# Sample-token matmuls of 32 and 64 columns, issued in alternation between column groups

## The chip, the cores and the metric

The kernel runs on one core of one Trainium2 chip. The metric is the device time of the whole program in microseconds (us); lower is better. Times of a stretch come from one profiled execution of the same program. PE is the matrix engine (TensorE), DVE, ACT and POOL are the vector, scalar and GpSimd engines, SP issues most transfers.

## The reference, cut to what matters

One inference step of a one-layer decoder for 1024 prompt tokens and for 8 sequences of 4 new tokens each (32 "sample" tokens). A layer adds three things to the stream: a token mixer (a gated delta rule with 4 heads beside local attention with windows 128, 512 and 2048 at strides 1, 4 and 16), cross-attention to 256 memory rows, and a mixture of tiny experts (PEER). For the sample tokens every sequence has its own state, its own window cache and its own memory rows:

```python
# gated delta rule, one token after another
S_t = a_t S_{t-1} + k_t u_t^T
u_t = beta_t (v_t - a_t S_{t-1}^T k_t)
o_t = S_t^T q_t
# local attention of the new tokens over the cache and themselves
s = einsum('bthc,btmhc->bhtm', q, kg) * dh**-0.5
p = exp(s - logsumexp(s));  o = einsum('bhtm,btmhc->bthc', p, vg)
# cross-attention
p = softmax(einsum('bthc,bmhc->bhtm', q, k_mem) * dh**-0.5)
o = einsum('bhtm,bmhc->bthc', p, v_mem)
```

So a product for the sample tokens has 8 parts (sequences, or positions of a window), each with its own key or value matrix. The kernel puts the queries of one part into a 32- or 64-column stationary tile that is zero elsewhere, and adds up 8 or 32 matmuls in one PSUM tile.

## The kernel before, in words

The prompt is worked in three groups of tokens (384, 384, 256); the sample tokens ride with the second group. `base` runs for each group: input norm and projections, then three rounds of delta-rule chunks (`delta_block`) and one window of local attention each (`windows(i)`), the output projection, cross-attention and the routing of the experts. After the third group a dense phase (`dense`) goes through all experts for part of the tokens. The experts of the other tokens are read row by row: `experts` and `experts_v` gather one row per token from HBM on POOL (L1248, tile `gat`, four buffers), and DVE multiplies it (L1257) or adds it up (L1406). These gathers run beside everything else, from about 700 us on. `mm` counts matmul work and notes a DVE instruction as an anchor each time enough of it has gone by; `paced` issues one gather step after each anchor.

The program is written in one order and then put in order engine by engine by a scheduler that follows a model of the times. Each engine's queue is fixed after that: an instruction that waits holds up what stands behind it on its engine. Tiles come from pools with fixed numbers of buffers that are taken in turn, and a load waits until the last reader of the buffer's old tile is done.

Four places touch the sample tokens' small matmuls. All operands are fp32; the trace shows two records for each such matmul.

- `delta_sample` (L629 to L677), once, about 1142 to 1192 us. For each of four heads: load the states `s` (512 KB, tile `zz`), 8 matmuls of 32 columns of the keys with the states into `r[:, 0]` (L657), DVE makes `x` (L660), one matmul gives `r[:, 1]` (L661), ACT copies it to `us` (L662), 8 matmuls of the queries with the states into `r[:, 2]` (L664), one more (L665), ACT copies it out (L666). Then eight 128-column matmuls make the new states (L672), which go back to HBM (L676). All of `r` that is used lies on partitions 0 to 31.
- `s_scores` (L921 to L949), once for each window. The four heads are two pairs; pair 0 fills partitions 0 to 63 of one PSUM tile (`tp`), pair 1 partitions 64 to 127. For windows 1 and 2 each pair has four steps `t8`: load 512 KB of keys into a `zz` tile (L938), make the stationary tile `z` (POOL memset L905, DVE copies L909), 8 matmuls of 64 columns (L941). Window 0 has one step for each pair. Pair 0 goes through all its steps, then pair 1.
- `win_sample` (L951 to L992), the same with values (L971, L975).
- `mem_sample` (L1095 to L1135): four heads, head `hd` on partitions `32*hd` to `32*hd+31`; for each of 8 sequences two halves of keys or values of 512 KB are loaded (L1144) into seven buffers (`O`, `wk`, `wv`), and 8 matmuls of 32 columns follow, the loop over heads outside and over the two halves of the sum inside.

`zz` has three buffers (`ZB = 3`), shared by the states, keys and values here. `halves_load` and `ztile` hand out the tiles.

## Time and profile before

| what | before |
|---|---|
| three runs | 4059.99, 4069.17, 4082.94 us |
| median | 4069.17 us |
| span of the profiled execution, first to last instruction | 4081.0 us |
| share of the span: PE, DVE, ACT, POOL | 89%, 72%, 36%, 36% |
| moved by DMA | 1101.38 MB, mean 270 GB/s |
| matmul records of PE | 18530 |

The profiled execution's own time is not given apart from its span; the slowest of the three runs is 1.9 us above that span, and the median 11.8 us below it. A busy share is an average over stages with different limits, so the stages are read one by one: the table of engines by stretch tells which engine is full, the groups by shape tell what a kind of matmul costs, the timelines tell what a matmul waited for, and the chain of waits tells whose work ended a stretch. In the lists, "x16" is 16 records, that is 8 fp32 matmuls, and a bracket at a row's end is idle time of the engine before that row with what ended it.

### The profile page before, as it was taken

To read this page: it belongs to the slowest core of one execution; us is meant where nothing else is said; L and a number is where in the kernel's file an instruction comes from. 1 tells how busy PE (TensorE), PEld (TensorE's weight loads), DVE (VectorE), ACT (ScalarE), POOL (GpSimd) and SP (SyncE) were. 2 spreads that over 40 slices of the span, in tenths; PEclk is the share of its full clock that TensorE was granted. 3 is DMA by queue.
4 is the path that set the end of the run, shared out by engine and by line. 5 is a ranking of instruction groups with operands and counts; after the bars stand their busy time and mean duration, and the time that the engine had idled before them with its cause. 6 is when DMAs were issued, how large, how long until landed. Compare 5 with 4: busy or idle time off the path is not lost.

```text
span 4081.0 us, 54174 instructions
## 1 busy us (share of the span) xinstructions
PE 3619.0 (89%) x18530; PEld 2976.6 (73%) x18530; DVE 2938.5 (72%) x6731; ACT 1470.6 (36%) x3278; POOL 1477.9 (36%) x1317
## 2 busy tenths in 40 slices
PE   8999988888999878774799887899969999999999
PEld 8988878666777634443677776788858888888887
DVE  4422338876575655789977887899768888887886
ACT  4434344333223011211245687223443333333333
POOL 0000000253334545454334443444544444444442
PEclk9998899789878988787788898999989999999998
DMA  6532554376668988886577888999999999999995
GB/s 219 188 117 92 189 196 146 123 254 206 230 229 298 334 331 310 296 297 201 189 237 267 290 321 330 327 349 330 348 323 336 342 342 340 340 339 321 338 332 198
DMA packets 383525, 1101.38 MB, mean 270 GB/s; under 512 B 40528, under 2 KB 147728, under 8 KB 379536
## 3 DMA queue, kind: packets, MB, share of 16 engines
q0 software_dynamic: 168736, 614.54, 42.5%
q1 hardware_dynamic: 214512, 483.37, 33.9%
q8 instruction: 147, 2.41, 0.2%
q14 instruction: 130, 1.06, 0.1%
HBM read 1025.37 MB, written 117.02 MB: 280 GB/s over the span
## 4 chain that ended last, share of the span: by engine, by line
PE 49%; DMA 18%; DVE 14%; issue 10%; POOL 4%; ACT 4%; POOLq 0%; SPq 0%; DVEq 0%; ACTq 0%
PE ps L148 29%; PE dl L148 11%; DMA gat<-expert_u,eid 5%; DMA gat<-expert_v,eid 5%; PE tp L148 4%; POOL gat L1248 4%; PE po L148 3%; DVE gat L1257 2%; DVE acc L1406 2%; DMA gat<-expert_v,e 1%; DMA O<-cmv 1%; PE tp L846 1%; DVE tk L1155 1%; DMA gscr<-C 1%; DVE tmp L419 1%
## 5 line engine op out<-in xcount | busy, mean ns | idle before, releaser
L1248 POOL DMA_INDIRECT gat<-expert_u,eid x512 | 625.1, 1221 | 819.1 <-DVE hid L1257 569.0
L1248 POOL DMA_INDIRECT gat<-expert_v,eid x512 | 627.7, 1226 | 771.8 <-DVE acc L1406 420.3
L1257 DVE CUSTOM_DVE_ANT_0 gat<-gat,fr 128x1024 f32<-128x1024 f32 x576 | 697.1, 1219 | 220.5 <-DMA gat<-expert_u,eid 209.2
L1406 DVE SCALAR_TENSOR_TENSOR acc<-gat,hid,acc 128x1024 f32<-128x1024 f32 x576 | 737.2, 1280 | 146.1 <-DMA gat<-expert_v,eid 128.9
L148 PE MATMUL dl<-dtm,dtm 128*128 128x128 f32 (+3 forms) x2336 | 328.2, 292 | 36.6 <-ACT C L1313 18.1
L148 PE MATMUL ps<-C,w 128*128 128x416 f32 x768 | 309.8, 562 | 43.2 <-DMA w<-w_pq 31.6
L148 PEld LDWEIGHTS dl<-dtm,dtm 128*128 128x128 f32 (+2 forms) x2336 | 307.7, 206 | 54.9 <-ACT C L1313 20.5
L148 PE MATMUL dl<-O,dtm 128*128 128x480 f32 x1152 | 286.3, 379 | 0.0
L148 PEld LDWEIGHTS ps<-C,w 128*128 128x128 f32 x768 | 156.7, 209 | 175.0 <-issue 127.3
L1266 ACT ACTIVATE dtm<-w 128x512 fp32r<-128x512 f32 x288 | 178.0, 629 | 269.7 <-PE dl L148 183.6
L148 PE MATMUL ps<-C,wk 128*128 128x480 f32 x1024 | 249.3, 385 | 21.2 <-ACT C L1266 12.7
L148 PE MATMUL ps<-C,zz 128*128 128x480 f32 (+1 forms) x1088 | 263.1, 379 | 1.4 <-DVE zz L1267 1.4
L1266 ACT ACTIVATE wk<-wv 128x1024 fp32r<-128x1024 f32 x128 | 135.8, 1061 | 332.9 <-PE ps L148 219.8
L148 PE MATMUL ps<-B,wk 128*128 128x480 f32 x1024 | 244.9, 381 | 0.2 <-DVE B L1267 0.2
L148 PEld LDWEIGHTS dl<-O,dtm 128*128 128x128 f32 x1152 | 216.6, 188 | 33.5
L148 PE MATMUL tp<-O,dtm 128*128 128x480 f32 x768 | 208.3, 386 | 32.1 <-ACT O L1266 30.1
L148 PEld LDWEIGHTS ps<-C,wk 128*128 128x128 f32 x1024 | 191.2, 190 | 56.4 <-ACT C L1266 13.6
L148 PEld LDWEIGHTS ps<-C,zz 128*128 128x128 f32 x1088 | 204.1, 188 | 32.3 <-DVE zz L1267 1.8
L1267 DVE TENSOR_TENSOR dtm<-w,dtm 128x512 fp32r<-128x512 f32 x288 | 197.0, 688 | 41.4 <-PE dl L148 16.8
L148 PE MATMUL ps<-A,w 128*128 128x256 f32 (+1 forms) x768 | 197.4, 415 | 21.2 <-ACT tmp L406 13.7
L148 PEld LDWEIGHTS ps<-B,wk 128*128 128x128 f32 x1024 | 193.8, 189 | 30.2 <-DVE B L1267 0.9
L148 PE MATMUL ps<-O,dtm 128*128 128x480 f32 x768 | 210.5, 379 | 0.2 <-DVE vzs L1394 0.2
(479 smaller groups left out, 6665.4 us busy)
## 6 DMA issues: line engine op xcount, KB each, us to landing
wv<-expert_uT SPq DMA_DIRECT2D x128, 512.0 KB
w<-expert_v SPq DMA_DIRECT2D x128, 512.0 KB
w<-w_in SPq DMA_DIRECT2D x102, 512.0 KB
s_win<-cache_win SPq DMA_DIRECT2D x64, 512.0 KB
A<-gscr SPq DMA_DIRECT2D x32, 960.0 KB
gscr<-C SPq DMA_DIRECT2D x13, 2048.0 KB
w<-w_pq SPq DMA_DIRECT2D x48, 512.0 KB
uscr<-tmp SPq DMA_DIRECT2D x60, 240.0 KB
```

What stands on the lines that cost most here:

```text
L148: x = self.nc.tensor.matmul(out, lhsT, rhs, **kw)
L419: nc.vector.scalar_tensor_tensor(av, xv(j), cw[:, ch, j:j + 1], av, op0=ALU.mult, op1=ALU.add)
L846: nc.tensor.transpose(tp[:r, c, :], e[:lq, j, o:o + r], C["ident"][:lq, :lq])
L1155: nc.vector.match_replace(out=w, in_to_replace=vals[:, 0:8], in_values=src, imm_value=-3.0e38)
L1248: return self.nc.gpsimd.indirect_dma_start(out=dst, out_offset=None, in_=src, in_offset=bass.IndirectOffsetOnAxis(ap=idx, axis=0))
L1257: nc.vector.tensor_tensor_reduce(out=u, in0=u, in1=fr, scale=1.0, scalar=0.0, op0=ALU.mult, op1=ALU.add, accum_out=hid[:, s:s + 1])
L1266: nc.scalar.activation(hi, x, AF.Copy)
L1267: nc.vector.tensor_tensor(lo, x, hi.bitcast(F32), op=ALU.subtract)
L1406: nc.vector.scalar_tensor_tensor(acc, v, c[:, s:s + 1], acc, op0=ALU.mult, op1=ALU.add)
```

## The change: what it does

It changes orders and one place in PSUM; no matmul, load or copy is added or taken away.

1. `delta_sample`: the queries' 8 matmuls now write partitions 32 to 63 of `r` and are issued alternately with the keys' 8, ahead of the DVE step.
2. `s_scores` and `win_sample`: the loop over the two pairs is inside the loop over the steps. Each step loads two tiles, makes two stationary tiles, and alternates the matmuls of the pairs.
3. `mem_sample`: the loop over the heads is inside the loop over the two halves of the sum.

```diff
@@ delta_sample
             for b in range(NB):
-                self.mm(r[:m, 0], kq[:, 0, b], s[:, b], start=b == 0, stop=b == NB - 1)
+                self.mm(r[:m, 0], kq[:, 0, b], s[:, b], start=b == 0, stop=b == NB - 1, skip_group_check=True)
+                self.mm(r[m:2 * m, 2], kq[:, 1, b], s[:, b], start=b == 0, stop=False, skip_group_check=True)
...
             nc.scalar.activation(us[:m], r[:m, 1], AF.Copy)
-            for b in range(NB):
-                self.mm(r[:m, 2], kq[:, 1, b], s[:, b], start=b == 0, stop=False)
-            self.mm(r[:m, 2], aT[:m, h], us[:m], start=False, stop=True)
-            nc.scalar.activation(on[:m, h], r[:m, 2], AF.Copy)
+            self.mm(r[m:2 * m, 2], aT[:m, h], us[:m], start=False, stop=True, skip_group_check=True)
+            nc.scalar.activation(on[:m, h], r[m:2 * m, 2], AF.Copy)
@@ s_scores
+        q = [wq[pr][:, L:] for pr in range(2)]
+        srcs = [[(hsl[hh], hh, x[hsl[hh]]) for hh in range(2)] for x in q]
+        for t8 in range(1 if g == 0 else 4):
+            kk, z = [], []
+            for pr in range(2):
+                kk.append(self.ztile())
+                nc.sync.dma_start(kk[pr], I["ck0"][pr] if g == 0 else I[f"ck{g}"][pr, t8])
+                z.append(self.diag_b(srcs[pr]) if g == 0 else self.diag(pr, t8, srcs[pr]))
+            for t in range(8):
+                for pr in range(2):
+                    self.mm(s[pr * DH:(pr + 1) * DH, :P], z[pr][:, t], kk[pr][:, t], start=t8 == 0 and t == 0, stop=False, skip_group_check=True)
         for pr in range(2):
-            rows = slice(pr * DH, (pr + 1) * DH)
-            q = wq[pr][:, L:]
-            srcs = [(hsl[hh], hh, q[hsl[hh]]) for hh in range(2)]
-            if g == 0:
...
-            else:
-                for t8 in range(4):
-                    kk = self.ztile()
-                    nc.sync.dma_start(kk, I[f"ck{g}"][pr, t8])
-                    z = self.diag(pr, t8, srcs)
-                    for t in range(8):
-                        self.mm(s[rows, :P], z[:, t], kk[:, t], start=t8 == 0 and t == 0, stop=False, skip_group_check=True)
...
@@ win_sample
+        for t8 in range(n8):
+            vv, z = [], []
+            for pr in range(2):
+                vv.append(self.ztile())
+                nc.sync.dma_start(vv[pr], I["cv0"][pr] if g == 0 else I[f"cv{g}"][pr, t8])
+                z.append(self.diag_b(srcs[pr]) if g == 0 else self.diag(pr, t8, srcs[pr]))
+            for t in range(8):
+                for pr in range(2):
+                    self.mm(op[rows[pr]], z[pr][:, t], vv[pr][:, t], start=False, stop=t8 == n8 - 1 and t == 7, skip_group_check=True)
@@ mem_sample, keys; the values likewise with m for c
-            for hd in range(4):
-                for c in range(2):
+            for c in range(2):
+                for hd in range(4):
                     self.mm(s[hd * NS:(hd + 1) * NS], qz[hd][:, c, b], ks[hd // 2][:, 2 * (hd % 2) + c, :],
                                      start=b == 0 and c == 0, stop=b == NB - 1 and c == 1, skip_group_check=True)
```

How it moves instructions, in three places. First PE in `delta_sample`, head 1 (tile `dl_8061` is its `r`, `zz_8056` its states, `dtm_8058` its masked keys and queries). Before:

```order
L148 MATMUL dl_8048<-dtm_8023,dtm_8046 128x128 x4
L148 MATMUL dl_8061<-zz_8056,dtm_8058 32x128 x8
L148 MATMUL dl_8061<-dtm_8070,dtm_7982 32x128
L148 MATMUL dl_8061<-zz_8056,dtm_8058 32x128 x8
L148 MATMUL dl_8061<-dtm_8070,dtm_7922 32x128
L148 MATMUL dl_8086<-dtm_8070,dtm_8084 128x128 x4
L148 MATMUL dl_8095<-dtm_8070,dtm_8093 128x128 x4
```

With the change:

```order
L148 MATMUL dl_8061<-zz_8056,dtm_8058 32x128 x16
L148 MATMUL ps_8630<-cf,ml_8604 64x128 x6
L148 MATMUL ps_8638<-cf,ml_8604 64x128 x6
L148 MATMUL dl_8061<-dtm_8078,dtm_7982 32x128
L148 MATMUL dl_8061<-dtm_8078,dtm_7922 32x128
L148 MATMUL dl_8086<-dtm_8078,dtm_8084 128x128 x4
L148 MATMUL dl_8095<-dtm_8078,dtm_8093 128x128 x4
```

The second group of eight has moved ahead of the one matmul that needs DVE's `x`, and nothing stands any more between that one and the one that needs ACT's `us`.

Second, PE in `s_scores` of window 2 (`tp_9623` is the scores' tile, each `zz` one loaded tile of keys, `ks` the new tokens' keys). Before:

```order
L148 MATMUL tp_9623<-zz_9624,tmp_9626 64x128 x8
L148 MATMUL tp_9623<-zz_9638,tmp_9640 64x128 x8
L148 MATMUL tp_9623<-zz_9652,tmp_9654 64x128 x6
L148 MATMUL ps_9589<-cf,ml_9579 64x128 x6
L148 MATMUL ps_9597<-cf,ml_9579 64x128 x6
L148 MATMUL tp_9623<-zz_9652,tmp_9654 64x128 x2
L148 MATMUL ps_9606<-cf,ml_9579 64x128 x6
L148 MATMUL ps_9614<-cf,ml_9579 64x128 x6
L148 MATMUL tp_9623<-zz_9666,tmp_9668 64x128 x8
```

With the change, from the last pair of the first two tiles on:

```order
L148 MATMUL tp_9623<-zz_9624,tmp_9626 64x128
L148 MATMUL tp_9623<-zz_9630,tmp_9632 64x128
L148 MATMUL tp_9623<-zz_9652,tmp_9654 64x128
L148 MATMUL ps_9589<-cf,ml_9579 64x128 x6
L148 MATMUL ps_9597<-cf,ml_9579 64x128 x6
L148 MATMUL ps_9606<-cf,ml_9579 64x128 x6
L148 MATMUL ps_9614<-cf,ml_9579 64x128 x6
L148 MATMUL tp_9623<-zz_9658,tmp_9660 64x128
```

Where three tiles were used up one after the other, two are now used up together, eight matmuls each in turn, and the third waits for a fourth.

Third, SP's loads and stores of `zz` tiles around the delta heads and window 1 (`s_delta` is the store of a head's new states, `ck` the keys). Before:

```order
L676 DMA s_delta<-zz_8056 128x1024
L938 DMA zz_8648<-ck 128x1024
L938 DMA zz_8662<-ck 128x1024
L676 DMA s_delta<-zz_8103 128x1024
L938 DMA zz_8676<-ck 128x1024
L938 DMA zz_8690<-ck 128x1024
L676 DMA s_delta<-zz_8150 128x1024
```

With the change:

```order
L675 DMA s_delta<-zz_8056 128x1024
L930 DMA zz_8648<-ck 128x1024
L675 DMA s_delta<-zz_8103 128x1024
L930 DMA zz_8654<-ck 128x1024
L675 DMA s_delta<-zz_8150 128x1024
L930 DMA zz_8676<-ck 128x1024
L930 DMA zz_8682<-ck 128x1024
```

The second tile of keys, which took the buffer of the first, now takes that of the third head's states and stands behind the store of those.

## Rows read from the trace of the kernel before

**Rows 1.** The page's head and its first part: the span, busy time of each engine.

```profile
span 4081.0 us, 54174 instructions
PE 3619.0 (89%) x18530; PEld 2976.6 (73%) x18530; DVE 2938.5 (72%) x6731; ACT 1470.6 (36%) x3278; POOL 1477.9 (36%) x1317
```

**Rows 2.** Engines by stretch: stretch and its length, busy us (records), clock share, DMA share, GB/s.

```profile
3300.00:3400.00 100.00, 100.00 (x464) 86.80 (x463) 84.91 (x111) 33.80 (x51) 41.66 (x38) 1.00 0.98 339
1210.00:1260.00 50.00, 50.00 (x306) 38.30 (x305) 32.49 (x53) 10.62 (x46) 26.28 (x29) 1.00 0.92 331
1376.00:1490.00 114.00, 103.12 (x323) 57.88 (x321) 75.48 (x80) 10.49 (x20) 59.40 (x49) 0.91 0.88 314
```

**Rows 3.** PE's groups by shape from 1142 to 1376: busy us, mean ns | idle before.

```profile
L148 PE MATMUL tp<-zz,tmp 128*64 128x128 f32 x512 | 67.2, 293 | 16.6 <-DMA zz<-ck 10.0 <-DMA zz<-cv 5.1 <-POOL tmp L905 1.5
...
L148 PE MATMUL dl<-zz,dtm 128*32 128x128 f32 x128 | 21.1, 335 | 0.7 <-ACT dtm L662 0.7
```

**Rows 4.** The chain of waits from 1376 to 1492, shares by line.

```profile
by line: DMA gat<-expert_v,eid 73.6%; issue 13.5%; POOL gat L1248 7.0%; DVE acc L1406 4.1%; PE po L148 1.4%; DVE dtm L1102 0.3%; DVE O L1008 0.3%; POOLq L1248 0.2%; DVEq L1406 0.1%
```

**Rows 5.** PE's timeline, third delta head: start, length, instruction, count [idle before].

```profile
1165.06 3.62 PE L148 MATMUL dl<-zz,dtm 128*32 128x128 f32 x16
1169.12 0.63 PE L148 MATMUL dl<-dtm,dtm 32*32 32x128 f32 x2 [0.43 <-DVE dtm L660]
1170.10 3.51 PE L148 MATMUL dl<-zz,dtm 128*32 128x128 f32 x16 [0.36 <-ACT dtm L662]
1173.55 2.38 PE L148 MATMUL dl<-dtm,dtm 32*32 32x128 f32 x18
```

**Rows 6.** PE's timeline, alternating groups: `win_merge`, then one head pair and four heads of `mem_sample`.

```profile
1145.97 1.56 PE L148 MATMUL ps<-cf,ml 128*64 128x128 f32 x24
1496.52 1.06 PE L148 MATMUL po<-O,dtm 128*32 128x256 f32 x8 [1.61 <-DMA O<-cmk]
1490.42 0.42 PE L148 MATMUL po<-O,dtm 128*32 128x256 f32 x3 [4.42 <-DVE dtm L1102]
1490.46 0.40 PE L148 MATMUL po<-wv,dtm 128*32 128x256 f32 x1
```

**Rows 7.** PE's timeline, values of window 0, then the end of window 1's scores.

```profile
1021.05 1.96 PE L148 MATMUL tp<-zz,tmp 128*64 128x128 f32 x16
1209.81 0.25 PE L148 MATMUL tp<-ks,tms 128*64 128x32 f32 x2
1210.11 1.13 PE L148 MATMUL dl<-cf,dtm 128*128 128x128 f32 x8
```

**Rows 8.** PE's timeline, window 2: scores from 1322, values from 1351.

```profile
1322.40 7.13 PE L148 MATMUL tp<-zz,tmp 128*64 128x128 f32 x43
1345.60 0.25 PE L148 MATMUL tp<-ks,tms 128*64 128x32 f32 x2
1351.22 6.92 PE L148 MATMUL tp<-zz,tmp 128*64 128x128 f32 x48 [1.51 <-POOL tmp L905]
1361.19 3.55 PE L148 MATMUL tp<-zz,tmp 128*64 128x128 f32 x16 [3.05 <-DMA zz<-cv]
1370.46 1.93 PE L148 MATMUL tp<-zz,tmp 128*64 128x128 f32 x16 [1.61 <-DMA zz<-cv]
1372.80 1.93 PE L148 MATMUL tp<-zz,tmp 128*64 128x128 f32 x16 [0.41 <-DMA zz<-cv]
```

**Rows 9.** SP's timeline: a store of states, the load after it, two loads of values.

```profile
1166.52 0.34 SPq L676 DMA_DIRECT2D s_delta<-zz  x1
1172.96 0.33 SPq L938 DMA_DIRECT2D zz<-ck  x1
1354.67 0.33 SPq L971 DMA_DIRECT2D zz<-cv  x1
1364.77 0.33 SPq L971 DMA_DIRECT2D zz<-cv  x1
```

**Rows 10.** Engines by stretch, columns as above, inside two of the 16-record pieces.

```profile
1361.20:1364.40 3.20, 3.20 (x15) 3.20 (x16) 1.79 (x2) 0.00 (x0) 0.94 (x1) 0.50 1.01 403
1370.50:1372.30 1.80, 1.80 (x16) 1.65 (x16) 0.25 (x2) 0.00 (x0) 1.50 (x2) 1.00 0.95 346
```

More of the change, by code (lines that the diff above doesn't have):

```diff
@@ L924, in s_scores @@
         hsl = [slice(hh * DH, (hh + 1) * DH) for hh in range(2)]
[L925 to L943 removed]
+        q = [wq[pr][:, L:] for pr in range(2)]
[9 more added lines that the diff above has]
+                    self.mm(s[pr * DH:(pr + 1) * DH, :P], z[pr][:, t], kk[pr][:, t], start=t8 == 0 and t == 0, stop=False, skip_group_check=True)
+        qd = []
+        for pr in range(2):
+            qd.append(self.tmp((P, 64)))
+            nc.gpsimd.memset(qd[pr], 0.0)
             for hh in range(2):
[L945 to L946 removed]
+                nc.vector.tensor_copy(qd[pr][hsl[hh], hh * NS:(hh + 1) * NS], q[pr][hsl[hh]])
+        for pr in range(2):
+            self.mm(s[pr * DH:(pr + 1) * DH, P:], qd[pr], ks[:, pr], start=False, stop=False, skip_group_check=True)
         self.mm(s[:, :P], self.identb, self.CB["wmS"][:, g * 160:g * 160 + P], start=False, stop=True, skip_group_check=True)
@@ L964, in win_sample @@
         allp = slice(0, P)
+        rows = [slice(pr * DH, (pr + 1) * DH) for pr in range(2)]
         for pr in range(2):
-            rows = slice(pr * DH, (pr + 1) * DH)
-            self.mm(op[rows], pn[:NS, 1, rows], vs[:NS, pr * P:(pr + 1) * P], start=True, stop=False, skip_group_check=True)
-            srcs = [(allp, hh, pn[:, 0, pr * DH + hh * NS:pr * DH + (hh + 1) * NS]) for hh in range(2)]
-            for t8 in range(1 if g == 0 else 4):
-                vv = self.ztile()
-                nc.sync.dma_start(vv, I["cv0"][pr] if g == 0 else I[f"cv{g}"][pr, t8])
-                z = self.diag_b(srcs) if g == 0 else self.diag(pr, t8, srcs)
-                last = g == 0 or t8 == 3
-                for t in range(8):
-                    self.mm(op[rows], z[:, t], vv[:, t], start=False, stop=last and t == 7, skip_group_check=True)
+            self.mm(op[rows[pr]], pn[:NS, 1, rows[pr]], vs[:NS, pr * P:(pr + 1) * P], start=True, stop=False, skip_group_check=True)
+        srcs = [[(allp, hh, pn[:, 0, pr * DH + hh * NS:pr * DH + (hh + 1) * NS]) for hh in range(2)] for pr in range(2)]
+        n8 = 1 if g == 0 else 4
+        for t8 in range(n8):
[5 more added lines that the diff above has]
+            for t in range(8):
+                for pr in range(2):
+                    self.mm(op[rows[pr]], z[pr][:, t], vv[pr][:, t], start=False, stop=t8 == n8 - 1 and t == 7, skip_group_check=True)
         O, M, d = run
@@ L1124, in mem_sample @@
             vs = self.halves_load(I["cmv"][b], b)
-            for hd in range(4):
-                for m in range(2):
+            for m in range(2):
+                for hd in range(4):
                     self.mm(o[hd * NS:(hd + 1) * NS], pz[hd][:, m, b], vs[m][:, hd], start=b == 0 and m == 0,
```

9 lines of the change are left out of this document (removed).

## The prediction

> **What bounds the kernel now.** I read the page's head first: PE is busy 89% of 4081.0 us, DVE 72% [rows 1]. Such shares are averages, so the engines by stretch came next. In the dense phase PE is full at the full clock (100.00 of 100 us, the 2.4 GHz level), with the transfers at 0.98 beside it [rows 2]. That phase is untouched, so what the change wins or loses before it moves it as a whole. The sample tokens' matmuls lie before 1566 us, in stretches with other limits: from 1210 to 1260 PE is full, and from 1376 to 1490 the chain of waits is 73.6% the landing of expert gathers, so PE does not set that stretch [rows 2, 4]. The groups by shape then size what is touched: the 64-column window matmuls take 67.2 us of PE between 1142 and 1376 and wait 16.6 us, nearly all for loads into `zz`; the 32-column ones of the delta heads take 21.1 us [rows 3]. Last, the timelines tell which of these matmuls had their data. The reader is to see there that the window matmuls come in bursts of 16 records with a load awaited between them [rows 8].
>
> **What alternation is worth.** The trace has matmuls that alternate between two column groups already: 24 records of `win_merge` took 1.56 us, 0.065 each, where a burst of 16 in one group took 1.93, 0.12 each [rows 6, 8]. So two groups run side by side, and I price an alternated pair of bursts at one burst: 1.93 us at the full clock, 3.55 at half (1.2 GHz) [rows 8, 10].
>
> **The change part by part**
>
> 1. *Delta heads.* In each head the queries' 16 records come after the wait for ACT, with nothing of their own to hide behind: 3.62, then 0.63, then 3.51 [rows 5]. They now run beside the keys' records. Half of 21.1 is 10.5 us [rows 3]; the waits for DVE (0.43) and ACT (0.36) stay. Taken −10. Bounds: −10.5, and 0 if later DVE work fills the gap.
>
> 2. *Window 0.* The values' two bursts of 1.96 become one: −1.9 [rows 7]. The scores' second stationary tile is late from DVE in either order: 0. Bounds −3.6 and 0.
>
> 3. *Window 1, scores.* They end at 1210.0 now; part 1 alone would make that 1200. But each pair now needs two tiles at once, and three buffers serve states and keys. The second tile of keys stands behind the store of the third head's states. That head ends at 1175.9 now, about 1168 then; a store took 6.4 us until its buffer could be loaded (1166.52 to 1172.96), a load 6 until its burst began (1354.67 to 1361.19 and 1364.77 to 1370.46: 6.5 and 5.7) [rows 8, 9]. So the first pair starts near 1180.5. From there a pair frees two buffers only at its end, one of which must be refilled before the next pair: 1.93 + 3 × (5.7 + 1.93) = 24.8, to 1205, and to 1210 with three pairs at the half clock. I take 1208: +8. The order puts 20 matmuls of the next delta chunk into these waits, 5 us at 1.13 for four [rows 7]: net +3. Bounds −5 and +10.
>
> 4. *Window 1, values.* PE is full there with other work between the bursts, which covers the loads: eight bursts become four, −7.7 [rows 2, 8]. Bounds −7.7 and 0.
>
> 5. *Window 2.* Nothing is left to fill PE. Now the scores last 23.4 us (1322.40 to 1345.85), and from there to the last value burst's end at 1374.7 are 28.9, of which 5.4 pass before the first burst [rows 8]. With the change and a wait W for each refill, scores take one burst and three times W plus a burst, values the same after 5.4. With W = 5.7 that is 24.8 and 30.2 at the full clock, together +2.7; at the half clock 31.3 and 36.7, +15.7. After a wait of 3.05 us the trace shows a burst at the half clock, after 1.61 and 0.41 at the full one [rows 8, 10]; W is longer, so I take +12, nearer the half clock. Bounds +2.7 and, at W = 7, +23.5.
>
> 6. *Cross-attention.* 0. Records of four heads start within 0.04 us of each other (three on `O` at 1490.42, `wv` at 1490.46) though twelve records stand ahead of the fourth head's first one in the order of before; and 8 records of two heads took 1.06 us [rows 6]. So PE has the overlap already. Keys' first halves are given back with the second ones, at most 1.06 us later for each of 8 sequences; the matmuls there wait for the transfers themselves (1.61), so I cost it at nothing; without that cover it is +8.
>
> 7. *Queues.* No transfer is added. POOL's memsets of stationary tiles go in pairs and hold gathers behind them; SP's weight loads stand behind waiting `zz` loads. The gathers' own chain covers both from 1376 on [rows 4]; before it they cost nothing as long as PE has other matmuls, as it has to 1322.
>
> On part 5, the Trainium skill's page "TensorE: Matmul & The Clock Gate", section "HAM oscillation — how this bites in real kernels", says that transfer waits between short bursts put the clock back, so that every burst starts cold. The trace agrees for the burst after 3.05 us [rows 8, 10]. By that rule all eight pairs of window 2 run at the half clock, and the sum below would be +3.7 higher.
>
> Sum: −10 − 1.9 + 3 − 7.7 + 12 = −4.6 us on 4081.0, so 4076.4. The median of the runs is 4069.17, 11.8 below that span; the same step from it gives **4064.6 us**. That is 0.1%, and a measurement of this kernel can tell about 0.5% (20 us) from no change: the forecast is no change that can be told.
>
> **The rivals**
>
> - *The tiles are there (faster).* If refills land sooner, because fewer are under way at a time, and the stretch keeps its filling work, the window matmuls halve: 67.2 / 2 = 33.6, with parts 1 and 2 −45: 4024; with half of the windows' share −29: 4040. For it: 1322.40 to 1329.5 runs 43 records without a wait. Against: every refill in rows 8 and 9 took 5.7 us or more.
> - *Refills take over (slower).* Pairs have one spare buffer where single tiles had two, so each pair pays the whole refill. At the half clock part 5 is 6 × W − 18.5. The sum passes +20 us where part 3 is at +10 and W reaches 8 us: then part 5 is +29.5 and the sum −19.6 + 10 + 29.5 = +20; at 8.5 it is +23, 4092. For it: the transfers are at 1.01 and 0.95 of their engines in these bursts [rows 10], and 6.5 us is seen. Against: refills under way are fewer, and gathers wait for DVE.
> - *Strict order (faster).* If PE began matmuls only in program order, only the seams between heads would overlap in cross-attention now: 13 steps for 16 records, against 8 with the change. A step is about 0.22 us (four in 1.06 with the last one's tail), so 5 × 0.22 × 16 = −17.6 more, −22 in all: 4047. Rows 6 speak against it as told. The Trainium skill states it on the same page, Part 3, section "The mechanism": matmuls start and end in the order of the program, and only weight loads are pulled ahead. The four starts within 0.04 us disagree with it.
> - *Nothing moves (same).* The two groups of a pair get no overlap where their tiles come late, or gathers on DVE's queue absorb either sign: 4069.
>
> **How the numbers follow.** Forecast 0.56, "the tiles are there" 0.17, strict order 0.03, refills 0.17, nothing moves 0.07. Faster by over 0.5% is 0.17 + 0.03 = 0.20, slower 0.17, within it 0.56 + 0.07 = 0.63. The range 4040 to 4096 reaches to the milder half of the first rival and just past the refill rival at 8.5 us; it leaves out the rest of both.
>
> **What would show it.** Right: kept counts of records; 32 records of states with 16 steps in a delta head, some 3.6 us at the half clock, and no second group after ACT; 32 records of a window pair within 2 us (or 3.6 at the half clock); waits of 5 to 7 us for `ck` and `cv` before three of four pairs in window 2, at a granted clock of 0.5; cross-attention's bursts as before; the dense phase as long as now and shifted by a few us. Wrong: pairs back to back in window 2 (first rival), waits of 8 us or more (second), cross-attention's stretch shorter by 10 us or more (third), or a move in the dense phase or in the expert routing around 1800, which I hold to be carried along; that would come from the order on DVE, which shifts by a few places.

## The result and the profile after

| | before | with the change |
|---|---|---|
| median of nine runs each | 4069.17 us | 4105.43 us |
| lowest to highest | 4059.99 to 4086.63 | 4085.35 to 4125.85 |
| ratio to before, 95% interval | | 1.0086 [1.0063, 1.0109] |
| time of the profiled execution | | 4092.87 us |

The change makes the kernel slower by 0.86%, 36 us by the medians. The forecast was 4064.6 in a range of 4040 to 4096: wrong in its sign and out of its range. The profiled execution of the change lies 13 us under its median, while that of before has a span 12 us above its median, so the two profiles are only 10 us apart and the stages have to be compared one by one. (One profile below, e3's, fell in an execution at a mean granted clock of 0.786 and isn't read, and the ratios leave such executions out; e7 is the same kernel at 0.893.)

The page's head and the line of the engines, after (to be held against [rows 1]):

```profile
span 4091.1 us, 54198 instructions
PE 3593.8 (88%) x18530; PEld 2956.7 (72%) x18530; DVE 2935.5 (72%) x6731; ACT 1473.3 (36%) x3278; POOL 1486.3 (36%) x1317
```

PE is busy 25 us less, in as many records, over a span that is 10 us longer: the matmuls were halved as planned, and waits took their place. PE's groups by shape from 1142 to 1400 us, after (columns as in [rows 3]):

```profile
L148 PE MATMUL tp<-zz,tmp 128*64 128x128 f32 x512 | 48.1, 351 | 39.7 <-DMA zz<-ck 20.3 <-DMA zz<-cv 9.8 <-DVE acc L1405 4.6
...
L148 PE MATMUL dl<-zz,dtm 128*32 128x128 f32 x128 | 10.9, 343 | 0.0
...
L148 PE MATMUL dl<-dtm,dtm 32*32 32x128 f32 x16 | 3.7, 314 | 7.6 <-DVE dtm L661 6.1 <-ACT dtm L663 1.1 <-DVE dtm L669 0.4
```

Before, the last of these groups read:

```profile
L148 PE MATMUL dl<-dtm,dtm 32*32 32x128 f32 x16 | 3.7, 314 | 2.4 <-DVE dtm L660 2.4
```

Against [rows 3] the window matmuls fell from 67.2 to 48.1 us, and PE's idle time ahead of them rose from 16.6 to 39.7. The delta heads' fell from 21.1 to 10.9, and the small matmuls behind them now wait 7.6 us instead of 2.4. (The wait put down to `acc` L1405 is the landing of a load as well: the tile of that pair was loaded at 1368.3 and its burst began at 1373.06.)

PE's timeline in window 2, after (columns as in [rows 5]):

```profile
1326.86 3.84 PE L148 MATMUL tp<-zz,tmp 128*64 128x128 f32 x34 [1.99 <-issue]
...
1335.76 1.92 PE L148 MATMUL tp<-zz,tmp 128*64 128x128 f32 x32
1343.45 3.68 PE L148 MATMUL tp<-zz,tmp 128*64 128x128 f32 x32 [5.77 <-DMA zz<-ck]
1352.82 3.43 PE L148 MATMUL tp<-zz,tmp 128*64 128x128 f32 x29 [5.69 <-DMA zz<-ck]
...
1364.99 3.52 PE L148 MATMUL tp<-zz,tmp 128*64 128x128 f32 x34 [2.76 <-POOL tmp L904]
1373.06 3.68 PE L148 MATMUL tp<-zz,tmp 128*64 128x128 f32 x32 [4.55 <-DVE acc L1405]
1382.18 3.26 PE L148 MATMUL tp<-zz,tmp 128*64 128x128 f32 x32 [5.44 <-DMA zz<-cv]
1389.75 3.65 PE L148 MATMUL tp<-zz,tmp 128*64 128x128 f32 x30 [4.31 <-DMA zz<-cv]
1400.62 0.45 PE L1003 MATMUL ps<-cf,tms 128*128 128x128 f32 x1 [7.22 <-DVE tms L1001]
```

A pair of 32 records takes 1.92 us, what 16 took before [rows 8]: two column groups do run side by side. But before five of the eight pairs PE waits 4.3 to 5.8 us for a load, and all pairs but the second run in 3.3 to 3.8 us. Engines by stretch inside the second and the third pair (columns as in [rows 2]):

```profile
1335.80:1337.60 1.80, 1.80 (x36) 1.63 (x30) 1.80 (x4) 0.00 (x0) 0.68 (x1) 1.00 1.03 389
1343.50:1347.00 3.50, 3.50 (x32) 3.23 (x32) 2.26 (x3) 0.00 (x0) 2.89 (x3) 0.50 0.81 282
```

The granted clock is 1.00 (2.4 GHz) where the pair followed other matmuls, and 0.50 (1.2 GHz) after 5.77 us without work. That is what the Trainium skill's page "TensorE: Matmul & The Clock Gate" says in "HAM oscillation — how this bites in real kernels"; the trace agrees.

Where the changed stretch loses its time, by PE's records at the same places of both profiles. Each row's time is counted from the first matmul of the delta heads (1142.42 and 1142.24 us).

| place (PE) | before | after | change so far |
|---|---|---|---|
| last new-state matmul of the delta heads ends | 49.1 | 36.4 | −12.8 |
| window 1's scores end (`tp<-cb`) | 67.8 | 70.0 | +2.2 |
| window 2's projections end (`ps<-cf,ks`) | 141.4 | 140.7 | −0.8 |
| the prompt's local attention ends (`ps<-cf,tmp` 8x8) | 180.0 | 182.6 | +2.6 |
| window 2's scores end | 203.6 | 214.6 | +11.0 |
| window 2's last value burst ends | 232.3 | 251.2 | +18.9 |
| first matmul of the output projection | 233.4 | 258.6 | +25.2 |

The last step, 6.3 us, is DVE's. DVE's timeline after (columns as before):

```profile
1392.64 1.29 DVE L1405 SCALAR_TENSOR_TENSOR acc<-gat,hid,acc 128x1024 f32<-128x1024 f32 x1 [2.76 <-DMA gat<-expert_v,eid]
1395.17 1.28 DVE L1405 SCALAR_TENSOR_TENSOR acc<-gat,hid,acc 128x1024 f32<-128x1024 f32 x1 [1.25 <-DMA gat<-expert_v,eid]
1397.47 1.28 DVE L1405 SCALAR_TENSOR_TENSOR acc<-gat,hid,acc 128x1024 f32<-128x1024 f32 x1 [1.01 <-DMA gat<-expert_v,eid]
1398.67 0.34 DVE L991 SCALAR_TENSOR_TENSOR so<-tp,small,so 128x128 f32<-128x128 f32 x1
...
1400.12 0.34 DVE L1001 SCALAR_TENSOR_TENSOR tms<-so,sd,cb 128x128 f32<-128x128 f32 x1
```

Window 2's values were done at 1393.4, but DVE's step on them, L991, stands behind three sums of gathered rows, two of which wait for rows that land later. In the kernel before, the wait at this place was 0.99 us.

Behind 1400 us this profile regains 18 us of the 25 up to the first `dl<-cf,gate` (2073 us before) and loses 20 from there to the last `ps<-tmp,B` (2436 us before), in the third group's token mixer and cross-attention; the experiments come back to that. The dense phase (first to last `tp<-O,dtm`) lasts 1031 us after and 1036 before.

### The profile page after: what moved, and what is told of

Its sections match the earlier page's. It is cut to its first block, busy times and chain, and to the rows that moved or that the text cites. A ratio compares the mean times of both kernels' runs of the same rounds, so it can differ in the third digit from the quotient of the medians.

```text
span 4091.1 us, 54198 instructions
## 1 busy us (share of the span) xinstructions
PE 3593.8 (88%) x18530; PEld 2956.7 (72%) x18530; DVE 2935.5 (72%) x6731; ACT 1473.3 (36%) x3278; POOL 1486.3 (36%) x1317
## 5 line engine op out<-in xcount | busy, mean ns | idle before, releaser
L1247 POOL DMA_INDIRECT gat<-expert_v,eid x512 | 646.5, 1263 | 770.4 <-DVE acc L1405 427.5
L1247 POOL DMA_INDIRECT gat<-expert_u,eid x512 | 614.2, 1200 | 839.9 <-DVE hid L1256 586.7
L1405 DVE SCALAR_TENSOR_TENSOR acc<-gat,hid,acc 128x1024 f32<-128x1024 f32 x576 | 737.1, 1280 | 160.5 <-DMA gat<-expert_v,eid 144.6
L148 PE MATMUL dl<-dtm,dtm 128*128 128x128 f32 (+3 forms) x2336 | 339.6, 298 | 50.8 <-ACT C L1312 24.4
L148 PEld LDWEIGHTS dl<-dtm,dtm 128*128 128x128 f32 (+2 forms) x2336 | 317.7, 211 | 71.3 <-ACT C L1312 27.3
```

What stands on the lines that cost most here:

```text
L148: x = self.nc.tensor.matmul(out, lhsT, rhs, **kw)
L1247: return self.nc.gpsimd.indirect_dma_start(out=dst, out_offset=None, in_=src, in_offset=bass.IndirectOffsetOnAxis(ap=idx, axis=0))
L1405: nc.vector.scalar_tensor_tensor(acc, v, c[:, s:s + 1], acc, op0=ALU.mult, op1=ALU.add)
```

## The experiments

Sixteen kernels in 18 runs. Times are ratios to the kernel before, measured on the same chip between the runs of each kernel, with 95% intervals. "Stretch" is the time from the first matmul of the delta heads to the first of the output projection in the run's profile, the length that the table above ends with.

| run | what it is | ratio | stretch, us |
|---|---|---|---|
| (the change) | all three parts | 1.0086 [1.0063, 1.0109] | 258.6 |
| e5 | before, against itself | 0.9999 [0.9977, 1.0021] | 235.2 |
| e1 | delta heads alone | 1.0054 [1.0030, 1.0077] | 236.3 |
| e2 | windows alone | 1.0087 [1.0058, 1.0117] | 255.2 |
| e8 | cross-attention alone | 1.0014 [0.9994, 1.0034] | 238.5 |
| e3, e7 | change, windows not alternated | 1.0101 [1.0065, 1.0137], 1.0117 [1.0089, 1.0145] | 241.2 (e7) |
| e4 | change, half tiles | 1.0026 [1.0004, 1.0048] | 227.2 |
| e6 | half tiles, windows alone | 1.0079 [1.0050, 1.0108] | 226.5 |
| e9 | change, old order held behind | 1.0044 [1.0019, 1.0068] | 250.8 |
| e10 | e1, old order held behind | 0.9993 [0.9971, 1.0015] | 223.0 |
| e11 | e4, old order held behind | 0.9995 [0.9976, 1.0015] | 228.1 |
| e12, t2 | e6, old order held behind | 0.9977 [0.9955, 0.9998], 0.9975 [0.9955, 0.9995] | 224.0, 227.8 |
| s1 | before, with the change's order behind | 1.0086 [1.0054, 1.0117] | 234.8 |
| s2 | e3, old order held behind | 0.9995 [0.9974, 1.0016] | 239.4 |
| s3 | change, DVE's order alone held | 1.0074 [1.0049, 1.0099] | 257.0 |
| s4 | e1, all other instructions held | 1.0009 [0.9989, 1.0029] | 231.5 |
| t1 | change, PE's order alone held | 1.0090 [1.0060, 1.0120] | 252.1 |

### One part at a time (e1, e2, e8) and before against itself (e5)

Each is the kernel before with the functions of one part taken from the change: `delta_sample` (e1), `s_scores` and `win_sample` (e2), `mem_sample` (e8). The short diffs are the three parts of the diff ahead of the prediction. The theory to be tested was that of the refills: a pair takes two of three buffers and gives them back together.

> The kernel before with part 1 alone (the delta heads' queries beside their keys); windows and cross-attention as before. Theory 'refills' (a pair takes two of the three zz buffers and gives them back together, so a transfer of 5 to 6 us stands ahead of each further pair; the windows lose the time): the 32-column matmuls fall from 21.1 to about 11 us and the windows are untouched, so 4069 falls to some 4060 (4055 to 4068). Theory 'delta on its own is worth nothing' (PE then waits for DVE's step L661, for which the trace of the changed kernel shows 5.9 us instead of 2.0): 4069, within 5 us. Theory 'the move of the order costs' (the delta heads' new order upsets what follows): 4080 or more.

> The kernel before with part 2 alone (both pairs of the windows together, matmuls alternated); delta heads and cross-attention as before. Theory 'refills': it carries the whole loss and the gain of the delta heads is missing, so 4069 rises by 36 to 46, to 4105 to 4115; PE's waits for ck and cv between 1142 and 1400 are 28 us or more (15.1 before). Theory 'the parts add up otherwise' (the loss needs the delta heads' early end, which lets window 1 run into late tiles): 4069 to 4085.

> The kernel before with part 3 alone (cross-attention's four heads inside, the two halves of the sum outside). Prediction's part 6 and 'refills': 4074, within 5 us; the order of DVE, POOL and SP is the same but for a handful of rows. 'Strict order' (PE begins matmuls only in program order): 17 us less, 4057. Theory 'order': 4074, as hardly anything is laid out anew.

> The kernel before, unchanged, against itself: how far two sets of runs and two profiled executions of one program lie apart. All theories: a ratio of 1.000 with an interval of 0.002 to either side, 4070 to 4078. What it tells apart: by 525 us, far ahead of the change, the profiles of the first and the fourth experiment were 7 us behind that of the kernel before; if this profile differs from the first by as much there, such shifts are the spread of single executions and no effect of an edit.

Measured: as "refills" had it, the windows alone come to 4113 us and wait 37.1 us for `ck` and `cv` (28 or more was forecast). The rest doesn't fit. The delta heads alone are 0.54% slower, where every theory but the third had a gain or nothing; the windows alone are 0.87% slower, as much as the whole change; cross-attention is 0.14% slower, with an interval that holds zero. The parts don't add up: 0.54 + 0.87 + 0.14 is 1.55, not 0.86. And the profile of e1 contradicts its own time: its stretch is 236.3 us, as before, so 22 us (0.54%) must come from elsewhere.

The kernel before against itself is 0.9999. Its second profile has a stretch of 235.2 us, and its first matmul of the second group's projections (`ps<-C,w`) at 761.62 us where the first has 754.87: single executions of one program wander by some 7 us before the changed place is reached, so the shifts of e1 and e4 there are no effect of an edit.

### Which property of the windows (e3 and e7, e4, e6)

e3 and e7 are one kernel, the change with the two inner loops exchanged:

```diff
-            for t in range(8):
-                for pr in range(2):
+            for pr in range(2):
+                for t in range(8):
```

e4 and e6 keep the alternation and change what a tile holds: four positions of both pairs. The host lays the caches out so; a load stays 512 KB.

```diff
-                    self.mm(s[pr * DH:(pr + 1) * DH, :P], z[pr][:, t], kk[pr][:, t], ...)
+                    k = kk[pr][:, t] if g == 0 else kk[t // 4][:, 4 * pr + t % 4]
+                    self.mm(s[pr * DH:(pr + 1) * DH, :P], z[pr][:, t], k, ...)
```

> The changed kernel with one thing undone: in the windows the eight matmuls of pair 0 are issued, then the eight of pair 1, not in alternation. Loads, stationary tiles and loop order stay those of the change; the first tile of a pair is needed alone and given back eight matmuls earlier. Theory 'refills': tiles are taken and given back one by one again, as in the kernel before, so window 2 lasts about as before (23.4 us of scores, 28.9 of values) and the time returns to 4060 to 4075. Theory 'order' (the loss comes from memsets in pairs on POOL, from loads in another order or from moved filling work, which all stay): 4095 to 4110, like the change. Theory 'short bursts' (the loss is the clock, which falls since alternation makes PE's work shorter): 4060 to 4075 too.

> The changed kernel with another content of a zz tile in windows 1 and 2: four positions of both pairs instead of eight of one (the cache lies so in HBM; as many loads, of as many bytes). The matmuls keep the change's alternated order, but each alternated group of eight now needs one tile and gives it back alone, so two buffers are under way as in the kernel before. Theory 'refills': the loss goes and the halved matmul time stays: 4069 falls by 10 to 25, to 4044 to 4059, and window 2's scores last under 22 us. Theory 'order': 4095 to 4110. Theory 'short bursts' (alternation itself leaves PE idle and at a granted clock of 0.5, whatever the buffers): 4080 or more, with the prompt's local attention ahead of window 2 at 0.5 as in the changed kernel (0.52 from 1284 to 1322).

> The kernel before with the windows of the fourth experiment (four positions of both pairs in one tile, alternated) and the delta heads and cross-attention of before. Theory 'late work' (the delta heads' gain is spent because matmuls that filled the stretch from 1285 to 1305 are issued earlier and that stretch then runs at a granted clock of 0.5; the windows with half tiles are a gain of their own): faster than the fourth experiment's 4087 and than before, 4055 to 4070. Theory 'order' (any edit here makes the scheduler lay out DVE and ACT anew for the stages behind, at 10 to 20 us): 4080 to 4095, like the fourth experiment. Theory 'refills' alone says 4060 to 4070.

> The third experiment's kernel once more, for a profile at the usual clock (the first one's mean granted clock was 0.786). Its time was 4114 where 'refills' had 4060 to 4075. If window 2 lasts as before (23.4 us of scores, 28.9 of values) and the loss stands elsewhere, the theory holds for window 2 but not for the time; if window 2 lasts 30 and 37 us as in the changed kernel, 'order' holds. Time by both: 4105 to 4120.

Measured, these runs seem to refute the refills: without alternation the kernel is no faster than the change (1.0101 and 1.0117), and half tiles alone give 1.0079, 4103 us, above the ranges of all three theories. e4's 4087 lies in the range of "short bursts", and its local attention ran at a granted clock of 0.59 and then 0.50; but with the old order held (e11, below) it runs at 0.57 and 0.50, and the kernel measures 0.9995. And the stretches say the opposite: 241.2 us in e7, 227.2 in e4 and 226.5 in e6, against 258.6 and 255.2 with full tiles in pairs. So the windows behave as the refills have it, and time is lost behind them. Counted from the start of the delta heads, e6 is 8.7 us ahead of before's second profile at the output projection, and 33 us behind it at the last matmul.

What differs there is the order. The scheduler lays out every queue by its model of the times, and another order in the windows moves thousands of later instructions. Ahead of the third group's cross-attention, 1000 us behind the change, DVE's two steps L314 and L316 of a norm stand like this in the second profile of before:

```profile
2349.91 0.17 DVE L314 TENSOR_REDUCE small<-ps 128x2 f32<-128x16 f32 x1
2351.57 0.17 DVE L316 RECIPROCAL small<-small 128x2 f32<-128x2 f32 x1 [1.49 <-ACT small L315]
```

and like this in the change:

```profile
2354.24 0.17 DVE L314 TENSOR_REDUCE small<-ps 128x2 f32<-128x16 f32 x1
2354.32 1.22 DVE L1256 CUSTOM_DVE_ANT_0 gat<-gat,fr 128x1024 f32<-128x1024 f32 x1
...
2355.46 2.17 DVE L1305 TENSOR_SCALAR dtm<-cb,i 128x128 f32<-128x128 bf16 x8
...
2360.77 1.22 DVE L1256 CUSTOM_DVE_ANT_0 gat<-gat,fr 128x1024 f32<-128x1024 f32 x1
...
2362.96 0.29 DVE L316 RECIPROCAL small<-small 128x2 f32<-128x2 f32 x1
```

Products of gathered rows and the preparation of other matmuls now stand between the two steps, which lie 8.7 us apart instead of 1.7. PE's timeline shows that PE pays for this one, first in before, then in the change:

```profile
2349.78 4.78 PE L148 MATMUL dl<-dtm,dtm 128*128 128x128 f32 x24 [0.85 <-ACT C L1313]
2354.39 0.61 PE L148 MATMUL ps<-cf,small 128*128 128x128 f32 x4
```

```profile
2357.20 1.16 PE L148 MATMUL dl<-dtm,dtm 128*128 128x128 f32 x8 [1.31 <-ACT C L1312]
2363.33 1.22 PE L148 MATMUL ps<-cf,small 128*128 128x128 f32 x4 [4.97 <-DVE small L316]
```

No matmul of this stage was edited.

### The order behind the change, held and exchanged (e9 to e12, s1 to s4, t1, t2)

To part the two, the queues behind the change were held to the order of the kernel before. Every instruction outside the edited functions exists in both kernels under the same number, so an edge between each two neighbours of the old order is enough; it orders the issue on one engine and carries no wait and no work.

```diff
+def queued(tc, nc):
+    at = {i.name: i for i in nc.cur_bb.bb.instructions}
+    row = np.frombuffer(zlib.decompress(base64.b85decode(ORDER)), np.int32)
+    for a, b in zip(row, row[1:]):
+        if a >= 0 and b >= 0:
+            tc.add_manual_dep(at[f"I-{b}"], f"I-{a}", mybir.DependencyInfo(mybir.DependencyClass.NoSync, mybir.DependencyReason.DATA), reason="order")
...
         hymba_kernel(tc, I, O)
+        queued(tc, nc)
```

`ORDER` holds the numbers, engine by engine, a negative one between engines: DVE, ACT, SP and POOL from 1376 us on and PE from 1578 on (e9 to e12, s2, t2); the change's order behind the same places in the kernel before (s1); DVE alone (s3), PE alone (t1), everything outside the edited functions from the start (s4).

> The changed kernel, but behind the changed stretch every engine's queue is held to the order that it has in the kernel before (DVE, ACT, SP and POOL from 1376 us on, PE from 1578 on, by ordering edges between neighbours that carry no wait; the changed functions' own instructions are left free). No work is added or removed. In the profile of the change, the stretch up to 1578 is 19 us longer than before. Theory 'local' (the whole loss arises in the changed stretch and is carried to the end): no difference to the change, 4100 to 4110 beside a before of 4070. Theory 'order' (the scheduler's new layout of the stages behind costs the rest): before plus 19, 4085 to 4095.

> The first experiment (delta heads alone, 0.54% slower than before) with the stages behind 1376 us held to the order of the kernel before, in the same way. Its profile was 4 us behind before at 1578 us, counted from the start of the delta heads, and 20 us behind at the end by the medians. Theory 'order': 4070 to 4079, no longer to be told from before. Theory 'local': 4088 to 4098 as in the first experiment.

> The fourth experiment (the whole change with half tiles, 0.26% slower than before) with the stages behind 1376 us held to the order of the kernel before. Its profile was 6 us ahead of before at 1578 us, counted from the start of the delta heads. Theory 'order': 4060 to 4069, faster than before by some 6 us (0.15%). Theory 'local': 4080 to 4090 as in the fourth experiment.

> The sixth experiment (windows with half tiles alone, 0.79% slower than before) with the stages behind 1376 us held to the order of the kernel before. Its profile was 6 us ahead of the second profile of before at 1578 us, counted from the start of the delta heads, and 28 us behind at the end. Theory 'order': 4060 to 4069. Theory 'local': 4095 to 4108 as in the sixth experiment.

> The kernel before, with none of the change, but behind 1376 us every engine's queue is held to the order of the changed kernel (DVE, ACT, SP, POOL from there, PE from the matmuls of cross-attention's output on). Theory 'order': this order costs time by itself, as much as holding the old order gave back to the change (4105 to 4089): 4070 rises by 10 to 20, to 4080 to 4090. Theory 'interplay' (the new order fits the change's own timing and hurts only with it): 4065 to 4076.

> The third experiment (the change's loop order and loads, but the matmuls of the two pairs not alternated; 1.1% slower than before) with the stages behind 1376 us held to the order of the kernel before. Theory 'refills and order' (tiles are given back one by one here, so nothing is left but the order): 4060 to 4074, and clearly under the 4089 that the change shows with the order held. Theory 'loads in pairs' (it is the loop order, with two stationary tiles and two loads at a time, that costs): 4085 to 4095.

> The changed kernel with DVE's queue alone held to the order of the kernel before from 1376 us on; PE, ACT, SP and POOL are laid out anew. Theory 'DVE's queue' (the sums of gathered rows stand ahead of the steps that PE waits for): as good as holding all five, 4085 to 4095. Theory 'several queues': between 4095 and 4105.

> The first experiment (delta heads alone) with every instruction outside the delta heads, windows' and cross-attention's own functions held to the order of the kernel before, from the start of the program. The matmuls of the next delta chunk stay where they fill the windows and the prompt's local attention. Prediction's part 1: the 10 us of PE are a gain where nothing takes their place: 4055 to 4066 (before 4070). Theory 'waits' (PE waits for DVE's step of each head instead, 5.9 us in the changed kernel): 4066 to 4075.

> The changed kernel with PE's queue alone held to the order of the kernel before, from the matmuls after cross-attention on (1578 us); DVE, ACT, SP and POOL are laid out anew. Theory 'PE's order': as good as holding all five, 4085 to 4095. Theory 'the queues have to agree' (an order on one engine fits only the orders on the others): 4098 to 4115, as with DVE alone.

> The twelfth experiment once more: half tiles in the windows, alternated, delta heads and cross-attention of before, order behind 1376 us held. If alternation gains where tiles come one by one (8 us at 1379 us in the first profile beyond the second profile of before), the ratio is again 0.996 to 0.999, 4058 to 4068 beside 4072; if the first set was spread, 0.999 to 1.002.

**The order costs about half.** With the old order held, the change measures 1.0044 instead of 1.0086, e1 0.9993 instead of 1.0054, e4 0.9995 instead of 1.0026, e6 0.9977 instead of 1.0079, e3 0.9995 instead of 1.0101. All five fall, by 0.3 to 1.2% (for the change it is 0.42%, give or take 0.34 by the two intervals, so "half" is rough); four of the five medians lie in the range that "order" gave, e10's 4 us below its. The other way round, the kernel before with the change's order and nothing of the change measures 1.0086, 4117 us by the median where 4080 to 4090 was expected. That isn't a clean sum (0.44% for the stretch and 0.86% for the order would make 1.30%). A likely reason, not tested, is that an order laid out for windows which end 25 us later hurts more where they end early. PE's timeline at the output projection, in before and then in s1:

```profile
1389.73 28.12 PE L148 MATMUL ps<-O,w 128*128 128x416 f32 x72 [5.32 <-DVE B L1045]
```

```profile
1367.59 8.55 PE L150 MATMUL ps<-O,w 128*128 128x416 f32 x24
1413.60 27.28 PE L150 MATMUL ps<-O,w 128*128 128x416 f32 x72 [37.46 <-DVE B L1047]
```

In s1 DVE's two additions of the output projection stand behind 22 sums of gathered rows, and PE waits 37.46 us for them, where it waited 5.32.

DVE's queue alone (s3) gives 1.0074, 4108 us, above the ranges of both its theories, and PE's alone (t1) 1.0090; all five give 1.0044. PE's alone is clearly worse than all five, but DVE's alone can't be told from either end: its interval reaches from 1.0049 to 1.0099. So that the queues have to agree is likely and not shown, and which instructions among them matter was not tried.

**What is left is the refills.** With the same order behind them, three kernels differ in the windows alone. Two tiles at once and alternated (e9): 1.0044. The same loads and loops but not alternated, so that tiles come and go one by one (s2): 0.9995. Alternated, one tile at a time (e11): 0.9995. It is neither the loop order nor alternation, but that alternation needs both tiles of a pair, and gives both back, at the same time: 0.49% (give or take 0.32), some 20 us. The stretch says the same in every profile: 250.8 to 258.6 us in the five with pairs of full tiles, 224.0 to 228.1 in the five with half tiles, 235.2 and 233.4 in two profiles of before (238.5 in e8, which has the same windows). Its last part, from the end of the prompt's local attention on, says it more sharply still: 69.7 to 76.0 us in the five with pairs, 51.4 to 55.1 in the fourteen others (e3 left out), whatever stands around the windows; e9 has 69.7 and s2 51.4.

PE's timeline in window 2 of e9 and of e12, scores:

```profile
1338.51 3.63 PE L150 MATMUL tp<-zz,tmp 128*64 128x128 f32 x32 [5.50 <-DMA zz<-ck]
1347.41 3.43 PE L150 MATMUL tp<-zz,tmp 128*64 128x128 f32 x29 [5.28 <-DMA zz<-ck]
```

```profile
1322.45 1.04 PE L150 MATMUL tp<-zz,tmp 128*64 128x128 f32 x16
1324.26 1.09 PE L150 MATMUL tp<-zz,tmp 128*64 128x128 f32 x16 [0.76 <-DMA zz<-ck]
1326.36 1.09 PE L150 MATMUL tp<-zz,tmp 128*64 128x128 f32 x16 [1.01 <-DMA zz<-ck]
1330.61 3.87 PE L150 MATMUL tp<-zz,tmp 128*64 128x128 f32 x32 [3.15 <-DMA zz<-ck]
```

With one tile per burst two loads are under way while a third tile is used up; the waits are 0.76, 1.01 and 3.15 us instead of 5 to 6, the short bursts keep the full clock, and of these four only the one after 3.15 us takes the long form, at a granted clock of 0.50.

**The delta heads' gain doesn't reach the end.** s4 has all other instructions at their old places and measures 1.0009, with an interval that leaves out the forecast 10 us (0.9975). PE's groups from 1142 to 1376, s4:

```profile
L150 PE MATMUL tp<-zz,tmp 128*64 128x128 f32 x512 | 70.8, 302 | 18.4 <-DMA zz<-ck 11.7 <-DMA zz<-cv 4.6 <-issue 1.9
...
L150 PE MATMUL dl<-zz,dtm 128*32 128x128 f32 x128 | 12.7, 381 | 0.0
...
L150 PE MATMUL dl<-dtm,dtm 32*32 32x128 f32 x16 | 3.7, 319 | 5.9 <-DVE dtm L663 4.8 <-ACT dtm L665 1.1
```

The heads' matmuls save 8.4 us against [rows 3] (21.1 to 12.7). The small matmuls behind them wait 5.9 us instead of 2.4, mostly for DVE's step, and the window matmuls take 3.6 us longer and wait 1.8 longer: 8.9 back in these two profiles. In e10, where the scheduler was free to use the earlier end of the heads, the stretch was 12 us shorter than before's second profile, but the time is 0.9993 [0.9971, 1.0015]. A gain of up to 0.3% there is neither shown nor excluded.

**A version that beats both.** e12 and t2 are one kernel: delta heads and cross-attention of before, windows alternated with half tiles, old order held behind. In two sets of runs it measures 0.9977 and 0.9975, both intervals under 1: about 10 us faster than before, and by the ratios 1.1% faster than the change.

## Why the prediction was wrong, point by point

Two steps failed. Parts 1, 3 and 4 counted matmul time saved on PE as time saved: they add up to −14.7 us, and at the end of the prompt's local attention the change was 2.6 us behind. And part 7 put the order of all that follows at nothing; it cost about as much as the windows.

- *Parts 1, 3 and 4 together.* By PE's records from the first matmul of the delta heads to the end of the local attention, the edited matmuls take 20.7 us less, as planned. But the other 747 records, none of them edited, take 11.5 us more, 7.1 of it in the local attention, which now runs at a granted clock of 0.50 nearly throughout; and PE waits 11.8 us longer (24.1 instead of 12.3). The prediction had no term for either.
- *Part 1, delta heads, −10.* PE's time fell as forecast (21.1 to 10.9 in the change). The last head ended 12.8 us earlier, but 8.6 of that are two bursts of window 1 with their waits, which stood ahead of it before (from 1176.54 and 1185.44 us) and now come after it. "Taken −10" failed in calling it a gain: the bound of 0 ("if later DVE work fills the gap") was the right end, as s4 shows. The waits for DVE, which were to stay, rose from 2.4 to 6.1 us in the change and to 4.8 in s4.
- *Part 2, window 0, −1.9.* The values' two bursts did become one, of 1.97 us; in the time it is not to be seen, as the start of the delta heads wanders by more from execution to execution.
- *Part 3, window 1's scores, +3.* The chain of loads was right, its size was not. The first pair started at 1181.4 (forecast 1180.5), but then what lay between the pairs took 7.0, 5.6 and 6.9 us instead of 5.7, and two of four pairs ran at the half clock. The scores ended at 1212.3 instead of 1208. The 20 matmuls of the next delta chunk did stand in these waits.
- *Part 4, window 1's values, −7.7.* Bursts halved, and every one of the four had its tiles. Only 3 us were gained up to the end of the projections, because the scheduler had moved matmuls of the third delta chunk ahead into this stretch. Where they had been, in the prompt's local attention, they left nothing to gain. Engines by stretch there, before and then after:

```profile
1285.50:1303.00 17.50, 16.36 (x109) 11.24 (x107) 14.25 (x25) 11.97 (x43) 8.25 (x7) 1.00 0.90 310
1303.00:1322.00 19.00, 18.00 (x80) 11.90 (x78) 5.92 (x11) 7.51 (x28) 2.64 (x5) 0.50 0.56 197
```

```profile
1288.00:1324.00 36.00, 33.65 (x136) 21.26 (x136) 11.15 (x14) 12.80 (x51) 8.02 (x10) 0.50 0.53 170
```

  Before, the attention's first part ran at 1.00 with the chunk's matmuls between (`dl<-Sst,B` at 1284.53 to `dl<-Sst,dtm` at 1292.51, which the change issues more than 20 us earlier), and its second part, almost without them, at 0.50; after, it ran at 0.50 nearly from its start. The stretch has less work and became 3.4 us longer. The prediction had both levels of the clock [rows 10] and applied them to the windows alone. That the missing matmuls are what lowered the clock fits these rows and was not tested by itself.
- *Part 5, window 2, +12.* Right: scores and values together took 14.2 us more from their first burst on (29.7 and 36.8 us against 23.4 and 28.9), waits were 4.3 to 5.8 us against the 5.7 taken, and the upper of the two sums, +15.7 at the half clock, was the nearer. The first rival, tiles that are there, is refuted, and so is its half.
- *Ahead of window 2 and behind it* the prediction had no term: PE stands idle for 1.99 us before the first burst, for nothing that the profile shows, and DVE's step behind three sums of gathered rows adds 6.3.
- *Part 6, cross-attention, 0.* Right: e8 is 1.0014 with zero in its interval. The "strict order" rival forecast −17.6 and is refuted by that run: PE had the overlap between heads before. (Two slips stand in the working and change nothing. The four records at 1490.4 are those of the last head of one sequence, for whose stationary tile PE had waited, and of three heads of the next, so ten records stand ahead of the last of them in the program, not twelve. And if both records of a matmul stand together, the rival's own counting gives 9 steps with the change and not 8, and so −14.)
- *Part 7 and the first paragraph.* Here the sign was lost. "What the change wins or loses before it moves it as a whole" holds for the dense phase, but not for the stages between 1400 us and it (expert routing and the third group): the order there was held to be carried along, with DVE's shift of a few places. It is laid out anew on the queues of PE, DVE and ACT. Of the 3737 DVE instructions that the `ORDER` of e9 and that of s1 both hold, 2733 stand at another place, by up to 64 places, and of PE's 8541 it is 1543. That costs about as much as the windows: 1.0086 falls to 1.0044 when the old order is held, and 1 rises to 1.0086 when the new one is put on the kernel before. Stage by stage the two parts can't be separated in the change's own profile, where most of the stretch's loss is regained by 2080 us and 20 us are lost behind it.
- *The rivals.* "Refills take over" named the mechanism of the measurable half, at 0.17, and put its price on waits of 8 us; they were 4.3 to 5.8. The stretch lost 25 us all the same, because parts 1, 3 and 4 gained nothing and some 8 us came ahead of window 2 and behind it. That an order a thousand microseconds away could decide was named only as the last of the things that would make the prediction wrong.

## What to carry to other kernels

Two operands that are used up in alternation are one operand to the buffers: count how many loads can be under way while a pair is in use, and put what is alternated into one tile rather than two. Where a scheduler orders the queues by a model, an edit is two changes, its own and a new order of all that follows; hold the old order behind the edit and measure both before believing either, and compare stages with the profiles of several executions. And matmul time saved in a stretch where others wait is no time saved: the local attention here lost its filling work and became longer.

## What the runs showed that was not expected

- Full use of PE doesn't go with its full clock: from 1303 to 1322 us in the kernel before PE is busy 18.00 of 19.00 us at a granted 0.50, from 1285.5 to 1303 16.36 of 17.50 at 1.00.
- One program's stages wander by more than an edit is worth: the same kernel took 363.2 us (e12) and 376.6 us (t2) from the first `dl<-cf,gate` to the last `ps<-tmp,B`. That stage took 360.7 to 365.2 in three profiles with the whole order of before, 361.6 to 376.6 in seven with that order held, 370.1 to 386.0 in eight without, and 412.0 in s1.
- Four starts within 0.04 us in the change's cross-attention as before it, whichever loop is outside, and no time gained: in this kernel, alternation shortened bursts where 16 records of one group had stood in a row, in the windows and the delta heads, and not where four had.
